# A Mamba-2 stage turned round: values as weights, and an order of four engines by hand

## The chip, the cores and the metric

The kernel runs on one core of one Trainium2 chip. The metric is the device time of one execution in microseconds (us), taken as the median of several runs. The profile comes from one execution that a hardware profiler recorded; its engines are PE (matrix products), PEld (loading of weights into PE), DVE, ACT and POOL (elementwise work) and SP (which issues most transfers).

## The reference

One layer of a bidirectional encoder of 1024 positions and 1024 channels. One projection makes the inputs of three branches (Mamba-2, RWKV-7 and HGRN2), which are merged by gates and followed by a feed-forward block. The change is in the Mamba-2 branch alone. All is float32.

```python
def ssd_chunked(x, dt, a, bm, cm):
    ...
    a_cum = jnp.cumsum(dt * a.reshape(G, hg), axis=2)
    xdt = x * dt[..., None]
    seg = a_cum[:, :, :, None] - a_cum[:, :, None]
    ...
    lmat = jnp.exp(jnp.where(mask, seg, -jnp.inf))
    cb = jnp.einsum('bcqgn,bcsgn->bcqsg', cm, bm)
    y_diag = jnp.einsum('bcqsgh,bcsghp->bcqghp', cb[..., None] * lmat, xdt)
    decay_to_end = jnp.exp(a_cum[:, :, -1:] - a_cum)
    chunk_states = jnp.einsum('bcsgn,bcsghp->bcghpn', bm, xdt * decay_to_end[..., None])
    ...
    y_off = jnp.einsum('bcqgn,bcghpn->bcqghp', cm, prev) * jnp.exp(a_cum)[..., None]
    return (y_diag + y_off).reshape(b, L, H, P)

def ssd_branch(z, xbc, dt_raw, conv_w, conv_b, dt_bias, a_log, d_skip, norm_w):
    ...
    y_f = ssd_chunked(xs, dt[:, :, 0], a[0], bm, cm)
    y_b = flip_t(ssd_chunked(flip_t(xs), flip_t(dt[:, :, 1]), a[1], flip_t(bm), flip_t(cm)))
    y = y_f + y_b + xs * d_skip[:, None]
    y = y.reshape(b, L, SSM_INNER) * jax.nn.silu(z)
    return rmsnorm(y, norm_w)
```

There are 16 heads of 64 values in two groups of 8 heads, a state of 128, and 8 chunks of 128 positions.

## The kernel before

The stages run in the order RWKV (`rwkv`), HGRN (`hgrn`), Mamba-2 (`ssd`), merge, feed-forward. The input projection has 79 column tiles. Each is a job (class `Jobs`) of 16 steps, and a step is three matmuls of 128x512 (L330 to L332: high part of the weights by high and low part of x, then low part of the weights by the high part of x). The first two jobs run at the start. The other 77, 3696 matmuls, are dealt out among the stages: `J.fill(n)` puts n steps at that place of the program, `J.share(w)` puts there the share w of what is left, out of `J.weight`, and `J.get` first completes the job whose result it reads. The weights of the stage stand in `FILL["ss"]`. A job also costs ACT a cast (L221) and copies of the result (L272), and DVE or POOL the low part of the weights (`wl`, L223).

A scheduler then makes one row of instructions for each engine. It may bring an instruction ahead of others where its inputs and buffers are there. Inside `tc.manual_schedule(engines=...)` the named engines keep the order of the program instead. Before the change that holds for POOL alone, and only in the chunk loop.

The stage (`ssd`, L1202 to L1438) begins with the step sizes `dt`, their cumulative sums (`cums`, and `cumd` in DRAM, one row for each head and direction) and decays to the chunk's end (`wst`, `dec`). Then, for each of two groups: six convolutions (`conv`: a load, an ACT operation, four DVE operations at L1298, a SiLU), of B, C and four tiles of values; scores `CB` = C·B for each chunk; and transposes (`xps`, L1345) of the values to position-major tiles `xt`.

The chunk loop of a group runs 8 times, with the forward direction at chunk i and the backward one at chunk 7 − i. `pairs` (two steps ahead) loads two exponent tiles of 8x128 per partition (`E<-cumd`), subtracts on POOL (L1368), picks one of the two by the triangle on DVE (L1371), takes exp on ACT and multiplies by `CB` (L1373). Then, for each direction, `yo` (L1389) multiplies C by the state, DVE scales it (`yt`, L1391), POOL adds it to `Y` (L1392); DVE makes weighted values `xw` (L1395), `st` (L1397) multiplies them by B, and POOL (L1401) and DVE (L1402) renew the state. `yd` (L1408) has each head's 128x128 exponent tile as weights and its 64 values as moving data, and L1410 adds it to `Y`, which is position-major. After the loop z is loaded, `Y` is transposed (`ytps`, L1428), gated by SiLU(z), stored in `ysc`, and its squares are summed in `ss`.

The E tiles, the convolutions' tiles and z's share five buffers (`EB`), and the loads of all of them stand in the queue of SP.

Of the kernel before, what the change touches and what calls it, by code (L numbers as in the profile page):

```python
# [9 lines left out]
F32 = mybir.dt.float32  # L10
# [8 lines left out]
P = 128  # L19
# [13 lines left out]
POOL = mybir.EngineType.Pool  # L33

# [5 lines left out]
    "ss": (4, 36, 12, 18, 6, 3, 8, 5, 22, 13, 8),  # L40
# [1161 lines left out]
def ssd(g, xr):  # L1202
# [3 lines left out]
    ysc = g.dram.tile([8, P, L], F32, tag="ysc", name="ysc")  # L1206
    cumd = g.dram.tile([32, L], F32, tag="cumd", name="cumd")
    ss = g.sspool.tile([P, L], F32, tag="ss", name="ss")

    J.weight = F[8] + 2 * F[0] + F[9] + F[10] + 2 * (F[1] + 4 * F[2] + F[3] + 16 * F[4] + 8 * F[5] + F[6] + 4 * F[7])  # L1210
    with ExitStack() as es:
# [12 lines left out]
        ecum = kp.tile([P, NT, 32], F32, tag="ecum", name="ecum")  # L1224
        wst = kp.tile([P, NT, 32], F32, tag="wst", name="wst")
        dec = kp.tile([P, NT, 32], F32, tag="dec", name="dec")
        with tc.tile_pool(name="s0t", bufs=1) as tp:
# [12 lines left out]
            J.share(F[8])  # L1240
# [29 lines left out]
            nc.scalar.activation(ecum, cums, AF.Exp)  # L1270
# [6 lines left out]
            nc.vector.tensor_sub(cums, cums, ld)  # L1277
# [7 lines left out]
        m8 = kp.tile([P, P], U8, tag="m8", name="m8")  # L1285
        nc.vector.tensor_copy(m8, mlt)

# [18 lines left out]
        for grp in range(2):  # L1306
            with ExitStack() as es2:
# [7 lines left out]
                J.share(F[1] + F[9] * grp)  # L1315

                cbd = yp.tile([P, NT], F32, tag="cbd", name="cbd")
                for h in range(2):
                    ps = pp.tile([P, 4, P], F32, tag="a", name="cbps", bufs=3)
                    ps2 = pp.tile([P, 4, P], F32, tag="a", name="btps", bufs=3)  # L1320
                    for j in range(4):
# [4 lines left out]
                    dg = yp.tile([P, 4, P], F32, tag="yt", name="dg", bufs=2)  # L1326
# [5 lines left out]
                nc.vector.tensor_tensor(gd, dtT[:, :, 16 + grp * 8:24 + grp * 8],  # L1332
                                        cbd.unsqueeze(2).broadcast_to([P, NT, 8]), MUL)
# [14 lines left out]
                Y = yp.tile([P, NT, 512], F32, tag="Y", name="Y")  # L1348
# [4 lines left out]
                def h3(t):  # L1353
                    return t.rearrange("p (h v) -> p h v", v=64)

                S = [yp.tile([P, 512], F32, tag=f"S{d}", name=f"S{d}") for d in range(2)]
                J.share(F[3])

                def pairs(c):

                    Es = []
                    for d in range(2):
                        e = sp.tile([P, L + 4], F32, tag="E", name="E", bufs=EB)
                        e = e[:, :L].rearrange("p (h t) -> p h t", t=P)
                        nc.sync.dma_start(e, cumd[d * 16 + grp * 8:d * 16 + grp * 8 + 8, c * P:(c + 1) * P]
                                          .unsqueeze(0).broadcast_to([P, 8, P]))
                        cs = cums[:, c, d * 16 + grp * 8:d * 16 + grp * 8 + 8]
                        nc.gpsimd.tensor_tensor(e, e, cs.unsqueeze(2).broadcast_to([P, 8, P]), SUB)  # L1368
                        Es.append(e)
                    e = Es[0]  # L1370
                    nc.vector.copy_predicated(e, m8.unsqueeze(1).broadcast_to([P, 8, P]), Es[1])  # L1371
                    nc.scalar.activation(e, e, AF.Exp)
                    nc.vector.tensor_mul(e, e, CB[:, c:c + 1, :].broadcast_to([P, 8, P]))  # L1373
                    return e

                order = ExitStack()
                order.enter_context(tc.manual_schedule(engines={POOL}))
                nxt = [pairs(0), pairs(1)]
                for i in range(NT):
                    if i < NT // 2:  # L1380
                        for c in (i, NT - 1 - i):
                            nc.gpsimd.tensor_tensor(h3(Y[:, c]), h3(xt[:, c]),
                                                    gd[:, c].unsqueeze(2).broadcast_to([P, 8, 64]), MUL)
                    e = nxt.pop(0)
                    for d in range(2):
                        c = i if d == 0 else NT - 1 - i
                        if i > 0:
                            ps = pp.tile([P, 512], F32, tag="b", name="yo", bufs=2)
                            nc.tensor.matmul(ps, CT[:, c * P:(c + 1) * P], S[d], start=True, stop=True)  # L1389
                            yt = yp.tile([P, 512], F32, tag="yt", name="yt", bufs=2)  # L1390
                            nc.vector.tensor_tensor(h3(yt), h3(ps), per_head(ecum, c, d), MUL)  # L1391
                            nc.gpsimd.tensor_add(Y[:, c], Y[:, c], yt)  # L1392
                        if i < NT - 1:
                            xw = yp.tile([P, 512], F32, tag="xw", name="xw", bufs=2)
                            nc.vector.tensor_tensor(h3(xw), h3(xt[:, c]), per_head(wst, c, d), MUL)  # L1395
                            ps = pp.tile([P, 512], F32, tag="b", name="st", bufs=2)
                            nc.tensor.matmul(ps, Bt[:, c], xw, start=True, stop=True)  # L1397
                            if i == 0:
                                nc.vector.tensor_copy(S[d], ps)
                            else:  # L1400
                                nc.gpsimd.tensor_tensor(h3(S[d]), h3(S[d]), per_head(dec, c, d), MUL)  # L1401
                                nc.vector.tensor_add(S[d], S[d], ps)  # L1402
                        if d == 0 and i + 2 < NT:
                            nxt.append(pairs(i + 2))
                        J.share(F[4])
# [729 lines left out]
```

## Time and profile before

| what | us |
|---|---|
| median of three runs | 2452.01 (2451.94 to 2453.88) |
| the profiled execution | 2453.83 |
| its span | 2452.1 |
| DVE busy in the span | 1611.1 |
| POOL busy in the span | 1078.3 |
| ACT busy in the span | 981.5 |

The span is the stretch from the first to the last instruction. A line of the profile gives the source line, the engine, the operation with the tile written and the tiles read, the count after an x, busy microseconds and mean nanoseconds, then the idle time of the engine before them and what ended it. In a timeline a row begins with start and length in us, and the brackets give the idle time before it and its releaser. A matmul in plain float32 leaves two records, one of the projection leaves one.

### The profile page before, as it was taken

How to read it: one execution, taken by the hardware profiler on the slowest of the kernel's cores; microseconds unless marked ns; L12 is line 12 of the kernel's file. 1: busy time of each engine (PE TensorE's matmuls, PEld its weight loads, DVE VectorE, ACT ScalarE, POOL GpSimd, SP SyncE). 2: the span in 40 equal slices, each digit the busy share in tenths (PEclk: the TensorE clock that was granted, in tenths of full speed). 3: DMA queues.
4: the chain of work that ended last, by engine and by line, in shares of the span. 5: the costliest groups of instructions: out<-in, count | busy, mean ns of one | idle time of the engine just before them, and what ended most of it. 6: DMA issues, size and time to landing. Idle time of an engine off the chain costs nothing.

```text
span 2452.1 us, 37480 instructions
## 1 busy us (share of the span) xinstructions
PE 2288.4 (93%) x14785; PEld 1847.8 (75%) x14785; DVE 1611.1 (66%) x2069; ACT 981.5 (40%) x1428; POOL 1078.3 (44%) x845
## 2 busy tenths in 40 slices
PE   8998999999988998999899889999899999999895
PEld 6776778788767877878668657788688888877674
DVE  5688763455569578546666776652774454479999
ACT  6554532222454655426224245332433333344333
POOL 4433422443136345310751771421464444447985
PEclk9999999999989999999899989999999999999998
DMA  5455685763442232225645646532232222253311
GB/s 150 122 144 133 165 214 123 223 193 109 148 144 87 87 117 74 80 83 173 148 119 169 146 149 212 191 114 76 61 103 87 78 86 86 79 179 116 100 60 69
DMA packets 381212, 306.23 MB, mean 125 GB/s; under 512 B 111273, under 2 KB 323149, under 8 KB 381037
## 3 DMA queue, kind: packets, MB, share of 16 engines
q1 hardware_dynamic: 260909, 225.71, 31.2%
q10 hardware_dynamic: 119936, 77.61, 10.8%
q8 instruction: 116, 1.90, 0.3%
q0 software_dynamic: 192, 0.52, 0.1%
q14 instruction: 59, 0.48, 0.1%
HBM read 209.68 MB, written 94.11 MB: 124 GB/s over the span
## 4 chain that ended last, share of the span: by engine, by line
PE 61%; DVE 23%; POOL 5%; issue 4%; DMA 3%; ACT 3%; SPq 0%; ACTq 0%; DVEq 0%; POOLq 0%
PE mm L330 7%; PE mm L331 7%; PE mm L332 7%; PE ps L1587 6%; PE ps L1589 6%; PE ps L1588 6%; DVE acc L1926 3%; DVE ab L1804 3%; PE mm L232 2%; PE mm L231 2%; PE mm L233 2%; DVE rb L1804 2%; POOL E L1368 2%; PE Gps L807 1%; DMA E<-cumd 1%
## 5 line engine op out<-in xcount | busy, mean ns | idle before, releaser
L330 PE MATMUL mm<-x,wh 128*128 128x512 f32 (+1 forms) x1232 | 500.1, 406 | 0.6 <-ACT wh L221 0.5
L331 PE MATMUL mm<-x,wh 128*128 128x512 f32 (+1 forms) x1232 | 494.4, 401 | 0.0
L332 PE MATMUL mm<-x,wl 128*128 128x512 f32 (+1 forms) x1232 | 492.3, 400 | 0.0
L330 PEld LDWEIGHTS mm<-x,wh 128*128 128x128 f32 (+1 forms) x1232 | 233.8, 190 | 61.9 <-issue 9.7
L332 PEld LDWEIGHTS mm<-x,wl 128*128 128x128 f32 (+1 forms) x1232 | 233.9, 190 | 55.1 <-issue 4.9
L331 PEld LDWEIGHTS mm<-x,wh 128*128 128x128 f32 (+1 forms) x1232 | 234.1, 190 | 53.7 <-issue 6.2
L1587 PE MATMUL ps<-xb,rb 128*128 128x512 f32 x432 | 168.0, 389 | 0.0
L1588 PE MATMUL ps<-xb,rb 128*128 128x512 f32 x432 | 168.0, 389 | 0.0
L1589 PE MATMUL ps<-xb,rb 128*128 128x512 f32 x432 | 167.9, 389 | 0.0
L1587 PE MATMUL ps<-rb,ab 128*128 128x512 f32 x308 | 125.5, 407 | 20.5 <-DVE acc L1926 19.5
L221 ACT CAST wh<-wr 128x1024 fp32r<-128x1024 f32 (+2 forms) x103 | 100.2, 972 | 101.9 <-PE mm L331 86.2
L223 POOL TENSOR_TENSOR wl<-wr,wh 128x1024 fp32r<-128x1024 f32 x30 | 78.9, 2630 | 133.6 <-ACT wh L221 123.1
L223 DVE TENSOR_TENSOR wl<-wr,wh 128x1024 fp32r<-128x1024 f32 (+2 forms) x73 | 98.5, 1349 | 49.6 <-ACT wh L221 49.4
L1588 PE MATMUL ps<-rb,ab 128*128 128x512 f32 x308 | 122.7, 398 | 2.3 <-POOL rb L1804 2.3
L1589 PE MATMUL ps<-rb,ab 128*128 128x512 f32 x308 | 121.5, 397 | 1.5 <-DVE ab L1804 1.5
L1751 ACT CAST rb<-fs 128x512 fp32r<-128x512 f32 x85 | 52.8, 622 | 166.1 <-PE ps L1589 117.8
L272 ACT COPY st<-mm 128x512 f32<-128x512 f32 x130 | 75.5, 582 | 93.2 <-PE mm L332 81.7
L810 DVE TENSOR_TENSOR Gc<-Gps,mk 128x256 f32<-128x256 f32 x64 | 27.2, 424 | 108.2 <-PE Gps L807 62.1
L231 PE MATMUL mm<-oh,wh 128*128 128x512 f32 x224 | 88.5, 397 | 6.1 <-DVE gt L1491 4.2
L1926 DVE TENSOR_TENSOR acc<-acc,ps 128x512 f32<-128x512 f32 x148 | 94.1, 674 | 0.0
L1588 PEld LDWEIGHTS ps<-xb,rb 128*128 128x128 f32 x432 | 81.1, 188 | 16.9
L1589 PEld LDWEIGHTS ps<-xb,rb 128*128 128x128 f32 x432 | 81.1, 188 | 16.8
(503 smaller groups left out, 5472.0 us busy)
## 6 DMA issues: line engine op xcount, KB each, us to landing
wr<-in_w_in_dram ACTq DMA_DIRECT2D x74, 512.0 KB
fr<-in_ffn_w_in_dram SPq DMA_DIRECT2D x44, 512.0 KB
E<-cumd SPq DMA_DIRECT2D x32, 512.0 KB
pg<-st ACTq DMA_DIRECT2D x48, 256.0 KB
gt<-pg SPq DMA_DIRECT2D x24, 512.0 KB
ad<-a SPq DMA_DIRECT2D x22, 512.0 KB
dr<-in_ffn_w_down_dram SPq DMA_DIRECT2D x22, 512.0 KB
ar<-ad SPq DMA_DIRECT2D x22, 512.0 KB
```

What stands on the lines that cost most here:

```text
L221: nc.scalar.copy(hi[:, :kt, :n], raw[:, :kt, :n])
L223: g.lo_eng.tensor_sub(lo[:, :kt, :n], raw[:, :kt, :n], f32(hi[:, :kt, :n]))
L231: nc.tensor.matmul(ps, whi[:, k, :n], xh, start=(k == 0), stop=False)
L272: g.nc.scalar.copy(st[:n], ps)
L330: g.nc.tensor.matmul(ps[:n], w[0][:, k, :n], xh, start=(k == 0), stop=False)
L331: g.nc.tensor.matmul(ps[:n], w[0][:, k, :n], xl, start=False, stop=False)
L332: g.nc.tensor.matmul(ps[:n], w[1][:, k, :n], xh, start=False, stop=(k == KT - 1))
L1587: nc.tensor.matmul(ps, ah, bh, start=(i == 0), stop=False)
L1588: nc.tensor.matmul(ps, ah, bl, start=False, stop=False)
L1589: nc.tensor.matmul(ps, al, bh, start=False, stop=(i == n - 1))
L1804: eng.tensor_sub(blk[:, 1], s, f32(blk[:, 0]))
L1926: nc.vector.tensor_add(m[j], m[j], ps)
```

## The change

Inside the stage, for each group:

- `yd` has the values as weights (128x64) and the exponent tile of the head as moving data (128 columns). Even heads write to the lower half of the partitions, odd heads to the upper. The result is feature-major: 128 partitions hold two heads' values, and the free axis has 4 pairs of heads by 128 positions. `yo` has quarters of the state as weights and C as moving data, so it has the same shape.
- So `Y`, the position-major scaling by `ecum` and the transposes at the end are gone. The feature-major scaling is `X`, the exp of half of the loaded rows (ACT), by which DVE multiplies `yo`. The D skip goes into the diagonal of the exponent tile, which a second copy_predicated (`id8`, `gd`) sets.
- z is loaded and SiLU'd ahead of the loop, stored in `zd`, and read back chunk by chunk (`gate`); `ysc` is stored chunk by chunk.
- The subtraction of `cums` from the two exponent tiles on POOL becomes eight ACT operations with a bias for the forward one, and stays on POOL for the backward one. The product of the state and `dec` moves from POOL to DVE.
- All seven backward states (`Sb`) are made first; then one loop over the chunks does both directions.
- From the first exponents to the loop's end, PE, ACT, DVE and POOL all keep the order of the program. The weights in `FILL["ss"]` are new.

```diff
-    "ss": (4, 36, 12, 18, 6, 3, 8, 5, 22, 13, 8),
+    "ss": (4, 30, 12, 5, 5, 14, 22, 8, 5),
...
-    J.weight = F[8] + 2 * F[0] + F[9] + F[10] + 2 * (F[1] + 4 * F[2] + F[3] + 16 * F[4] + 8 * F[5] + F[6] + 4 * F[7])
+    J.weight = F[6] + 2 * F[0] + F[7] + F[8] + 2 * (F[1] + 4 * F[2] + 7 * F[3] + 8 * F[4] + 8 * F[5])
...
-            nc.vector.tensor_sub(cums, cums, ld)
+            nc.vector.tensor_sub(cums, ld, cums)
...
+        m8, id8 = (kp.tile([P, P], U8, tag=n, name=n) for n in ("m8", "id8"))
         nc.vector.tensor_copy(m8, mlt)
+        nc.vector.tensor_copy(id8, g.ident)
...
+                nc.vector.tensor_add(gd, dtT[:, :, grp * 8:grp * 8 + 8], dtT[:, :, 16 + grp * 8:24 + grp * 8])
+                nc.vector.tensor_tensor(gd, gd, cbd.unsqueeze(2).broadcast_to([P, NT, 8]), MUL)
...
-                Y = yp.tile([P, NT, 512], F32, tag="Y", name="Y")
+                for q in range(grp * 4, grp * 4 + 4):
+                    zs = sp.tile([P, L + 4], F32, tag="E", name="zs", bufs=EB)[:, :L]
+                    nc.sync.dma_start(zs, J.get(g.pz, q))
+                    nc.scalar.activation(zs, zs, AF.Silu)
+                    nc.sync.dma_start(zd[q], zs)
...
-                def pairs(c):
...
+                        h0 = d * 16 + grp * 8
+                        nc.sync.dma_start(e, cumd[h0:h0 + 8, c * P:(c + 1) * P].unsqueeze(0).broadcast_to([P, 8, P]))
                         Es.append(e)
+                    return Es
+                def exponents(c, Es):
+                    Xs = []
+                    for d in (1, 0):
+                        e, h0 = Es[d], d * 16 + grp * 8
+                        X = yp.tile([P, 4, P], F32, tag=f"X{d}", name="X", bufs=2)
+                        if c != (0, NT - 1)[d]:
+                            for b in range(2):
+                                hr = slice(b * 64, b * 64 + 64)
+                                nc.scalar.activation(X[hr], e[hr, b::2], AF.Exp)
+                        cs = cums[:, c, h0:h0 + 8]
+                        if d == 0:
+                            for h in range(8):
+                                nc.scalar.activation(e[:, h], e[:, h], AF.Identity, bias=cs[:, h:h + 1])
+                        else:
+                            nc.gpsimd.tensor_tensor(e, e, cs.unsqueeze(2).broadcast_to([P, 8, P]), ADD)
+                        Xs.insert(0, X)
+                    return Xs
+                def pick(Es):
+                    nc.vector.copy_predicated(Es[0], m8.unsqueeze(1).broadcast_to([P, 8, P]), Es[1])
+                def decays(c, e):
+                    nc.scalar.activation(e, e, AF.Exp)
+                    yield
+                    nc.vector.tensor_mul(e, e, CB[:, c:c + 1, :].broadcast_to([P, 8, P]))
+                    nc.vector.copy_predicated(e, id8.unsqueeze(1).broadcast_to([P, 8, P]),
+                                              gd[:, c].unsqueeze(2).broadcast_to([P, 8, P]))
+                    yield
+                def gate(c):
+                    z = yp.tile([P, 4, P], F32, tag="z", name="z", bufs=2)
+                    nc.sync.dma_start(z, zd[grp * 4:grp * 4 + 4, :, c * P:(c + 1) * P].rearrange("q p t -> p q t"))
+                    return z
...
+                Sb = yp.tile([P, NT - 1, 512], F32, tag="Sb", name="Sb")
+                Sa = yp.tile([P, 512], F32, tag="Sa", name="Sa")
+                def weighted(d, c):
+                    xw = yp.tile([P, 512], F32, tag="xw", name="xw", bufs=2)
+                    nc.vector.tensor_tensor(h3(xw), h3(xt[:, c]), per_head(wst, c, d), MUL)
+                    return xw
+                def update(d, c, xw, old, new):
+                    ps = pp.tile([P, 512], F32, tag="b", name="st", bufs=2)
+                    nc.tensor.matmul(ps, Bt[:, c], xw, start=True, stop=True)
+                    if old is None:
+                        nc.vector.tensor_copy(new, ps)
+                    else:
+                        nc.vector.tensor_tensor(h3(new), h3(old), per_head(dec, c, d), MUL)
+                        nc.vector.tensor_add(new, new, ps)
+                order = ExitStack()
+                order.enter_context(tc.manual_schedule(engines={PE, ACT, DVE, POOL}))
+                Es = rows(0)
+                X, z = exponents(0, Es), gate(0)
+                ahead = rows(1)
+                xw = weighted(1, NT - 1)
+                pick(Es)
+                for _ in decays(0, Es[0]):
+                    pass
+                for c in range(NT - 1, 0, -1):
+                    xn = weighted(1, c - 1) if c > 1 else weighted(0, 0)
+                    update(1, c, xw, Sb[:, c] if c < NT - 1 else None, Sb[:, c - 1])
+                    xw = xn
+                    J.share(F[3])
+                for i in range(NT):
+                    ts = slice(i * P, (i + 1) * P)
+                    nEs = ahead
+                    if i + 2 < NT:
+                        ahead = rows(i + 2)
+                    if i + 1 < NT:
+                        nX, nz = exponents(i + 1, nEs), gate(i + 1)
+                    part = []
+                    for d, S in ((1, Sb[:, i] if i < NT - 1 else None), (0, Sa if i else None)):
+                        if S is None:
+                            continue
+                        ps = pp.tile([P, 4, P], F32, tag="b", name="yo", bufs=2)
+                        for q in range(4):
+                            nc.tensor.matmul(ps[:, q], S[:, q * P:(q + 1) * P], CT[:, ts], start=True, stop=True)
+                        nc.vector.tensor_mul(X[d], X[d], ps)
+                        part.append(X[d])
+                    if i < NT - 1:
+                        update(0, i, xw, Sa if i else None, Sa)
+                    J.share(F[4])
...
+                    ps = pp.tile([P, 4, P], F32, tag="a", name="yd", bufs=3)
                     for h in range(8):
-                        nc.tensor.matmul(ps[:, h], e[:, h], xt[:, i, h * 64:h * 64 + 64],
+                        nc.tensor.matmul(ps[h % 2 * 64:h % 2 * 64 + 64, h // 2], xt[:, i, h * 64:h * 64 + 64], e[:, h],
                                          start=True, stop=True)
-                    nc.vector.tensor_add(Y[:, i], Y[:, i], ps.rearrange("p h v -> p (h v)"))
+                    y = part[0]
+                    if len(part) > 1:
+                        nc.vector.tensor_add(y, y, part[1])
+                    nc.vector.tensor_add(y, y, ps)
+                    nc.vector.tensor_mul(z, z, y)
+                    nc.sync.dma_start(ysc[grp * 4:grp * 4 + 4, :, ts].rearrange("q p t -> p q t"), z)
...
+                    nc.scalar.activation(y, z, AF.Square)
+                    nxt = iter(())
+                    if i + 1 < NT:
+                        pick(nEs)
+                        nxt = decays(i + 1, nEs[0])
+                        next(nxt)
+                    if i + 2 < NT:
+                        xw = weighted(0, i + 1)
+                    eng = nc.vector if grp and i == NT - 1 else nc.gpsimd
+                    eng.tensor_add(y[:, 0:2], y[:, 0:2], y[:, 2:4])
+                    if grp == 0:
+                        eng.tensor_add(ss[:, ts], y[:, 0], y[:, 1])
+                    else:
+                        eng.tensor_add(y[:, 0], y[:, 0], y[:, 1])
+                        eng.tensor_add(ss[:, ts], ss[:, ts], y[:, 0])
+                    next(nxt, None)
                     J.share(F[5])
+                    if i + 1 < NT:
+                        Es, X, z = nEs, nX, nz
```

The rows of PE, up to the last product of HGRN's states (`sps`), are the same before and after. The next place is in the setup of group 0, where the step sizes are transposed (`dtps`; `mm` is a matmul of the projection). Before, on PE:

```order
L330 MATMUL mm<-x_373,wh 128x512
L1246 MATMUL dtps<-ident,dt 128x32 x8
L331 MATMUL mm<-x_374,wh 128x512
L332 MATMUL mm<-x_373,wl 128x512
L330 MATMUL mm<-x_382,wh 128x512
L331 MATMUL mm<-x_383,wh 128x512
L332 MATMUL mm<-x_382,wl 128x512
L330 MATMUL mm<-x_391,wh 128x512
L1246 MATMUL dtps<-ident,dA 128x32 x8
```

The same place after, on PE, with the norm of HGRN's last head (`nps`) ahead of it:

```order
L179 MATMUL nps<-t,ones 128x512
L180 MATMUL nps<-t,ones 128x512
L1247 MATMUL dtps<-ident,dt 128x32 x8
L1247 MATMUL dtps<-ident,dA 128x32 x8
L1258 MATMUL rps<-tri_le,dAT 32x128 x4
L1258 MATMUL rps<-tri_ge,dAT 32x128 x4
```

No matmul of the projection stands there any more. The end of that setup, on PE, after: the last scores and transposes, the first product of a backward state (`st`), and behind it the first projection matmuls since HGRN's `sps`:

```order
L1324 MATMUL cbps<-CT,BT 128x128 x4
L1325 MATMUL btps<-ident,BT 128x128 x4
L1346 MATMUL xps<-ident,xq 128x128 x32
L1420 MATMUL st<-xw,Bt 128x512
L331 MATMUL mm<-x_217,wh 128x512
L332 MATMUL mm<-x_218,wh 128x512
L333 MATMUL mm<-x_217,wl 128x512
```

Counted over PE's rows, 2562 projection matmuls stood ahead of that `sps` before and 2553 after. Ahead of the first `st` stood 3055 before, and 2553 after; the others moved behind it.

The last place is the start of the chunk loop of group 0, on DVE. Before:

```order
L1395 TENSOR_TENSOR xw<-xt,wst 128x512
L1371 COPY_PREDICATED E<-m_10226,E 128x1024
L1395 TENSOR_TENSOR xw<-xt,wst 128x512
L1373 TENSOR_TENSOR E<-E,CB 128x1024
L1371 COPY_PREDICATED E<-m_10226,E 128x1024
L1399 COPY S_10668<-st 128x512
```

After, with `id` the mask of the diagonal and `Sb` the backward states:

```order
L1415 TENSOR_TENSOR xw<-xt,wst 128x512
L1393 COPY_PREDICATED E<-m_10222,E 128x1024
L1399 TENSOR_TENSOR E<-E,CB 128x1024
L1400 COPY_PREDICATED E<-id_10223,gd 128x1024
L1415 TENSOR_TENSOR xw<-xt,wst 128x512
L1422 COPY Sb<-st 128x512
```

The second weighted values, which the second `st` needs, stand behind the whole exponent tile of chunk 0 now, with the new operation on the diagonal among it; before, only the pick stood between them.

77 lines of the change are left out of this document (6 added, 71 removed).

## The prediction

> **What bounds the kernel now.** I read the page first: its share of busy time and the chain that ended last.
>
> ```profile
> span 2452.1 us, 37480 instructions
> ...
> PE 61%; DVE 23%; POOL 5%; issue 4%; DMA 3%; ACT 3%; SPq 0%; ACTq 0%; DVEq 0%; POOLq 0%
> ```
>
> PE ends the chain for 61% of the span, so the Mamba-2 stage must be judged by what PE loses in it. I cut the stage into stretches: from the last HGRN state matmuls at 1022 us to the first use of the exponents (1173.3), the chunk loop of group 0, the setup of group 1, its loop, and the start of the merge. The columns are the engines' busy time (and instructions), the granted TensorE clock, the DMA share and GB/s.
>
> ```profile
> core 0: us, PE busy (x) PEld busy (x) DVE busy (x) ACT busy (x) POOL busy (x), PEclk, DMA share, GB/s
> 1022.00:1173.30 151.30, 146.12 (x918) 122.34 (x917) 82.58 (x95) 66.53 (x87) 26.41 (x30) 0.98 0.39 118
> 1173.30:1285.00 111.70, 99.43 (x410) 71.30 (x409) 77.26 (x70) 26.49 (x30) 79.84 (x48) 0.91 0.55 131
> 1285.00:1366.00 81.00, 81.00 (x403) 68.22 (x402) 52.75 (x48) 39.36 (x49) 13.89 (x18) 1.00 0.54 167
> 1366.00:1461.90 95.90, 75.66 (x289) 49.90 (x287) 72.25 (x67) 27.95 (x30) 78.00 (x47) 0.84 0.54 139
> 1461.90:1500.00 38.10, 38.09 (x177) 31.95 (x178) 28.37 (x34) 20.05 (x23) 5.04 (x3) 0.96 0.78 268
> sum 478.00, PE 440.30 PEld 343.72 DVE 313.21 ACT 180.38 POOL 203.19; mean PE 88.06 PEld 68.74 DVE 62.64 ACT 36.08 POOL 40.64
> ```
>
> In both setups PE is full although almost nothing of the stage itself runs on it: 146 of 151 us and 81 of 81. What fills it are the projection jobs. In the two loops PE waits and its clock falls, while POOL is busy 80 of 112 us and 78 of 96. The work by line, same 478 us, and the true step of a matmul:
>
> ```profile
> L331 PE MATMUL mm<-x,wh 128*128 128x512 f32 x381 | 156.5, 411 | 0.0
> L330 PE MATMUL mm<-x,wh 128*128 128x512 f32 x381 | 156.3, 410 | 0.0
> L332 PE MATMUL mm<-x,wl 128*128 128x512 f32 x382 | 154.9, 406 | 0.0
> L1389 PE MATMUL yo<-S,CT 128*128 128x512 f32 x56 | 37.0, 752 | 20.0 <-DVE S L1399 12.3 <-DVE yt L1391 5.5 <-DVE S L1402 2.1
> L1408 PE MATMUL yd<-xt,E 128*128 128x64 f32 x256 | 36.2, 295 | 0.0
> L1397 PE MATMUL st<-xw,Bt 128*128 128x512 f32 x56 | 33.5, 682 | 10.7 <-DVE yt L1391 5.3 <-DVE S L1402 3.0 <-DVE S L1399 2.2
> L231 PE MATMUL mm<-oh,wh 128*128 128x512 f32 x49 | 19.3, 401 | 1.9 <-ACT oh L1466 1.9
> L1428 PE MATMUL ytps<-ident,Y 128*128 128x128 f32 x64 | 9.1, 295 | 0.0
> ...
> 1165.15 0.39 PE L332 MATMUL mm<-x,wl 128*128 128x512 f32 x1
> 1165.37 0.39 PE L330 MATMUL mm<-x,wh 128*128 128x512 f32 x1
> ...
> 1277.33 1.02 PE L1389 MATMUL yo<-S,CT 128*128 128x512 f32 x2
> 1177.80 1.89 PE L1408 MATMUL yd<-xt,E 128*128 128x64 f32 x16
> 1024.00 3.29 PE L1145 MATMUL sps<-Vt,t 128*128 128x128 f32 x28
> ```
>
> Records overlap: a projection matmul lasts 0.39 us but the next one starts 0.23 later (0.2275 over long runs), so 0.16 of every length is overlap. A yo or st (two records each) then takes 0.86, a yd (two records) 0.23, a 128x128 record 0.11. Work at full clock: 1144 projection records and 145 of the merge (three lines, 49 the first) by 0.2275 = 293 us; yo and st 112 by 0.43 = 48; yd 256 by 0.116 = 30; ytps 64 by 0.11 = 7; the rest of the 2197 records, scores, transposes and HGRN's last products, about 36. Sum 414. The stretch lasts 478, so **PE loses 64 us now**: 38 idle by the sum row, the rest at a low clock.
>
> **The change, part by part.** It removes PE work and POOL work, and it moves projection work. Less PE work first. The 64 ytps records go: −7 us. Then yd gets weights of 64 columns (the values) in place of 128, in alternate halves of the array, with 128 moving columns in place of 64. The nearest row has such halves:
>
> ```profile
> 1055.01 1.15 PE L1108 MATMUL vps<-lv 128*64 128x64 f32 x32
> 1056.09 0.50 PE L332 MATMUL mm<-x,wl 128*128 128x512 f32 x1
> ```
>
> These are 16 matmuls of 64 moving columns (two records each), and the next matmul starts 1.08 us after them, so each takes 0.0675; 128 moving columns double that to 0.135, my value. The lower bound is 0.107, the upper 0.22, as for a 128x128 matmul (two records by 0.11) with no overlap of halves. 128 matmuls by 0.23 − 0.135 is −12 us, with −16 and −1 as the ends. By the Trainium skill, "TensorEngine Tiling (Array Packing)", section Performance Considerations, a weight of at most 64 columns allows up to twice the rate; the vps row agrees, and by that rule the term would be 0.107 and −15, three us from mine. y_off by quarters of S moves as many columns as before: ±0. New PE sum: 414 − 19 = **395**.
>
> Now the move. Until HGRN's last sps the rows of PE are the same, and 2553 projection matmuls of 3696 have been issued there (2562 before). Before, the scheduler then put 293 more ahead of the first dtps and 493 ahead of the first st (3055). With the change that number is 0: PE is one of the ordered engines now, later jobs belong behind the loop's first st, and nothing may cross it. So PE has only the stage's own chain from 1022 until the backward pass gets going, and 114 us of projection (about 500 by 0.2275) that ran there must run later. How long is that starved chain? Rows of the present setup, with what they waited for in brackets:
>
> ```profile
> 1066.12 0.74 DVE L1162 COPY_PREDICATED scd<-msk,vps 128x512 f32<-128x512 uint8 x1 [5.35 <-PE vps L1108]
> 1078.09 0.75 DVE L1184 SCALAR_TENSOR_TENSOR t<-ops,vcolsv,gg 128x512 f32<-128x512 f32 x1 [5.13 <-PE ops L1181]
> 1086.67 0.75 DVE L1184 SCALAR_TENSOR_TENSOR t<-ops,vcolsv,gg 128x512 f32<-128x512 f32 x1 [5.48 <-PE ops L1181]
> 1097.84 0.69 DVE L1196 TENSOR_TENSOR t<-t 128x512 f32<-128x512 f32 x1 [6.25 <-ACT t L1195]
> ...
> 1110.23 1.29 DVE L1298 SCALAR_TENSOR_TENSOR acc<-pt,vcolsv,acc 128x1024 f32<-128x1024 f32 x1 [3.09 <-ACT acc L1296]
> 1155.82 5.32 DVE L1298 SCALAR_TENSOR_TENSOR acc<-pt,vcolsv,acc 128x1024 f32<-128x1024 f32 x4 [0.89 <-ACT acc L1296]
> 1161.17 1.06 ACT L1300 ACTIVATE xq<-acc 128x1024 f32<-128x1024 f32 x1 [0.46 <-DVE acc L1298]
> 1166.43 1.23 DVE L223 TENSOR_TENSOR wl<-wr,wh 128x1024 fp32r<-128x1024 f32 x1 [5.30 <-ACT wh L221]
> 1164.57 1.90 POOL L1368 TENSOR_TENSOR E<-E,cums 128x1024 f32<-128x1024 f32 x1 [15.23 <-DMA E<-cumd]
> 1171.37 1.90 POOL L1368 TENSOR_TENSOR E<-E,cums 128x1024 f32<-128x1024 f32 x1 [4.90 <-DMA E<-cumd]
> 1173.30 1.32 DVE L1371 COPY_PREDICATED E<-m,E 128x1024 f32<-128x1024 uint8 x1 [4.38 <-POOL E L1368]
> ...
> 1162.26 18.70 DMA E<-cumd
> ```
>
> HGRN's tail runs from 1024.0 to 1098.5, 74.5 us. The first three rows wait 16 us for PE, whose own matmuls there last 1 to 3 us and sit between projection matmuls; with the smaller waits I take off 24, so 50. From there to the first conv operation it takes 11.7 us for loads, unchanged. The convs run from 1110.2 to 1161.1, 50.9 us; five wl splits of 1.23 leave DVE and some waits behind projection go, so 43. From the last conv to the first st (now 12) transposes no longer queue behind projection: 7. First st at 1024 + 112 = about 1136. There PE would be free, but DVE's rows now stand as follows: first weighted values, then pick, the product with CB and the diagonal of chunk 0, and only then the values of the second st. Those need both exponent tiles. Their loads now stand on SP behind four z loads, and the second behind a z store that frees its buffer; the load in the last row took 18.7 us. I put the end of the second load at 1145 (an estimate: loads land 6.8 us apart in the two L1368 rows, and a z store goes ahead of this one). Then come half the tile's exp twice, 1.2, the biases, 1.9 (POOL's L1368 row for the same sum), pick, 1.3 (the COPY_PREDICATED row), exp, 1.1 (ACT's row of 128x1024), the product and the diagonal, 1.2 and 1.3 (DVE's rows of 128x1024), and the values, 0.7: **second st at about 1155**. PE work in these 133 us is about 32 (30 of the rest, the first st, little of projection): **101 us lost**. Bounds: 1137 with the loads in time, or 1167 as slow as now.
>
> The clock falls in such stretches: the rows of the loops have 0.91 and 0.84 with gaps of a few us. The Trainium skill, "TensorE: Matmul & The Clock Gate", Part 1, has the clock halved after an idle window of about 3.4 us; the rows agree. By it, the 32 us of PE work in the starved stretch would cost up to twice, at worst +12 if the chain waits for all of it.
>
> Afterwards there is more projection than before: 471, 201 and 471 matmuls in group 0's loop, group 1's setup and its loop. A chunk has 46 of them (10.5), st 0.86, yo 1.7, yd 1.1: 14.2 us of PE. DVE has two or three products with yo and sums, gating, pick, exponents, and wl:
>
> ```profile
> L1395 DVE TENSOR_TENSOR xw<-xt,wst 128x512 f32<-128x512 f32 x13 | 19.8, 1524 | 0.0
> L1371 DVE COPY_PREDICATED E<-m,E 128x1024 f32<-128x1024 uint8 x8 | 17.5, 2186 | 18.0 <-POOL E L1368 18.0
> ...
> L1368 POOL TENSOR_TENSOR E<-E,cums 128x1024 f32<-128x1024 f32 x14 | 30.5, 2196 | 7.9 <-DMA E<-cumd 7.9
> L1392 POOL TENSOR_TENSOR Y<-Y,yt 128x512 f32<-128x512 f32 x14 | 19.7, 1410 | 19.5 <-DVE yt L1391 19.5
> ```
>
> Beside a busy POOL, xw takes 1.52 and pick 2.19; alone, 0.68 and 1.32 (1173.30). POOL loses the S and Y operations and one of two exponents: 3.5 us of a chunk are left, so most of DVE runs at the short length: seven of 0.69, one 0.7, 1.3, 1.2, 1.3 and 1.2 for wl, 10.5 to 12. That, ACT's eight small biases and two half exponents (8 of 14), and z and ysc by DMA (512 KB a chunk more; the last window carried 268 GB/s) lie beside PE; if PE's cover went, the excess over 14.2 would show. I add 6 for waits at the loops' ends, 2 for the clock after the starved stretch, 2 at the merge: 10.
>
> **Sum.** 395 + 101 + 10 = 506 against 478: +28. The profiled execution lasted 2453.83 (span 2452.1), and the median of the three runs is 1.8 lower, 2452.01. I put +28 on the median: **2480 us**. Own range: 2452 (loads in time, loops without loss, yd at 0.107) to 2515 (yd at 0.22, +11; starved stretch +12; POOL contention on DVE half the time, +12).
>
> **Rivals.** First, **DVE binds the loops**: every operation at its length beside POOL makes 18 us of a chunk against 14.2, 16 chunks by 3.7 = +59: 2539. For it speaks that the pick row had POOL beside it; against it that POOL loses two thirds of its time.
>
> Second, **faster**, the other side: the starved stretch is mostly PE's own queue delay. If tail and convs shorten further and the exponents are ready, the second st comes by 1125: 395 + 71 + 4 = 470, −8: 2444. The loops' old loss of 64 us really goes, so this decides as soon as the second st is before about 1130. Against it speaks DVE: its 82.6 busy us in the first stretch are nearly all chain, and the loads come on top.
>
> Third, **no change**: a second st between 1130 and 1137 with small losses, 2452; PE has merely lost elsewhere what it lost in the loops.
>
> **How the numbers follow.** Forecast 0.60, DVE bound 0.10, faster 0.20, no change 0.10. One measurement here tells about 0.2%, 5 us. Faster 0.20, same 0.10, slower 0.70. The range goes from 2440, which takes in the second rival, to 2520; it leaves out the first.
>
> **What would show it.** The PE row of the starved stretch: some 30 us busy in 130, clock well under 1, and no projection lines between sps and st. The second st near 1155, its idle ended by DVE's xw; behind it pick ended by a load. In the loops PE above 95%, xw at 0.7, 14 us a chunk, yd's eight matmuls in 1.1. It is wrong if the second st starts before 1137, if loop chunks take 18 us with PE waiting for DVE, or if yd still takes 1.9.

## The result, and the profile after

The changed kernel takes 2593.8 us (median of 4 runs, 2589.61 to 2596.09), the kernel before 2452.41: ratio 1.0574, 95% interval 1.0555 to 1.0592, or +141 us where +28 was forecast. The sign was right, the size was not, and the time lies outside the range.

The page's span and the chain that ended last, by engine:

```profile
span 2594.0 us, 37935 instructions
...
PE 54%; DVE 25%; DMA 8%; ACT 5%; issue 5%; POOL 2%; SPq 1%; ACTq 0%; DVEq 0%; POOLq 0%
```

PE's share of the chain fell from 61 to 54%, and transfers rose from 3 to 8. The windows of the changed kernel are cut at its own events: second st (1172.3), first yd (1202.9), last yd of group 0 (1338.4), second st of group 1 (1422.1), first and last yd of group 1. Columns as in the prediction.

```profile
core 0: us, PE busy (x) PEld busy (x) DVE busy (x) ACT busy (x) POOL busy (x), PEclk, DMA share, GB/s
1022.00:1172.30 150.30, 53.32 (x443) 44.94 (x441) 77.55 (x92) 53.57 (x73) 26.70 (x29) 0.62 0.33 87
1172.30:1202.90 30.60, 28.19 (x108) 20.02 (x108) 14.50 (x22) 8.37 (x17) 2.04 (x1) 0.95 0.36 89
1202.90:1338.40 135.50, 113.03 (x573) 88.64 (x572) 83.34 (x87) 60.61 (x110) 27.44 (x26) 0.90 0.52 129
1338.40:1422.10 83.70, 69.11 (x319) 56.86 (x320) 38.67 (x39) 36.75 (x53) 4.29 (x9) 0.90 0.62 174
1422.10:1451.60 29.50, 26.66 (x109) 19.12 (x107) 13.94 (x21) 8.37 (x17) 2.04 (x1) 1.00 0.35 92
1451.60:1588.60 137.00, 110.18 (x573) 86.44 (x572) 77.39 (x80) 55.37 (x106) 34.19 (x27) 0.91 0.45 122
```

The setup of group 0 is starved as forecast: PE busy for 53 of 150 us, at a clock of 0.62, where it was 146 of 151. What was not forecast are the two loops: 136 and 137 us, PE idle for 22 and 27 of them and at 0.90 and 0.91 of its clock on average, and no other engine near full.

For all kernels of this study I made one count: the records of PE in a stage times the unit prices of the prediction (0.2275 a projection matmul, 0.43 for 512 columns of a two-record product, 0.116 and 0.0675 a yd record before and after). A stage's length less that work is what PE **lost** there. A setup ends at the second st (or, before the change, at the second st of the loop), and the backward pass is counted with it.

| us lost by PE | setup 0 and backward pass | loop 0 | setup 1 and backward pass | loop 1 | sum |
|---|---|---|---|---|---|
| before | 8 | 21 | 0 | 29 | 58 |
| changed kernel | 120 | 36 | 20 | 37 | 213 |

The kernel before runs one more st and four yo behind its last yd of group 1 and loses 5 more there, so its stage loses 63 in all (the 64 of the prediction). That makes 150 more lost in the stage. The first 49 us of the merge lose 8 more than before (10 against 2), and PE has 17 us less work by the same count. 150 + 8 − 17 = 141, as measured. A stage's length is its work and its loss by definition, so this sum shows no cause; it says where the time went.

Against the kernel before, 112 came in setup 0, 20 in setup 1 and 18 in the loops. Against the forecast the loops stand out. Of the 113 us by which it was short, about 19 lie in setup 0 (120 against 101), 20 in setup 1 (none forecast) and 73 in the loops and the merge's start (83 against the 10 forecast for both).

### The profile page after: what moved, and what is told of

Read it like the earlier page. It is cut to its first block, busy times and chain, and to the rows that moved or that the text cites. A ratio compares the mean times of both kernels' runs of the same rounds, so it can differ in the third digit from the quotient of the medians.

```text
span 2594.0 us, 37935 instructions
## 1 busy us (share of the span) xinstructions
PE 2292.0 (88%) x14889; PEld 1856.7 (72%) x14889; DVE 1626.0 (63%) x2125; ACT 1045.4 (40%) x1610; POOL 970.4 (37%) x793
## 4 chain that ended last, share of the span: by engine, by line
PE 54%; DVE 25%; DMA 8%; ACT 5%; issue 5%; POOL 2%; SPq 1%; ACTq 0%; DVEq 0%; POOLq 0%
PE ps L1643 6%; PE ps L1645 6%; PE ps L1644 6%; PE mm L331 6%; PE mm L332 5%; PE mm L333 5%; DMA wr<-in_w_in_dram 3%; DVE ab L1860 2%; DVE acc L1982 2%; PE mm L232 2%; PE mm L233 2%; PE mm L234 2%; DVE wl L224 1%; DVE lv L1045 1%; DVE rb L1860 1%
## 5 line engine op out<-in xcount | busy, mean ns | idle before, releaser
L331 PE MATMUL mm<-x,wh 128*128 128x512 f32 (+1 forms) x1232 | 516.9, 420 | 0.6 <-ACT wh L222 0.5
L332 PE MATMUL mm<-x,wh 128*128 128x512 f32 (+1 forms) x1232 | 492.8, 400 | 0.0
L331 PEld LDWEIGHTS mm<-x,wh 128*128 128x128 f32 (+1 forms) x1232 | 237.3, 193 | 68.9 <-issue 16.6
L332 PEld LDWEIGHTS mm<-x,wh 128*128 128x128 f32 (+1 forms) x1232 | 237.0, 192 | 57.4 <-issue 9.9
L224 DVE TENSOR_TENSOR wl<-wr,wh 128x1024 fp32r<-128x1024 f32 (+2 forms) x73 | 91.7, 1257 | 163.0 <-ACT wh L222 152.8
L1420 PE MATMUL st<-xw,Bt 128*128 128x512 f32 x56 | 40.0, 804 | 92.5 <-DVE X L1455 47.6
L1387 POOL TENSOR_TENSOR E<-E,cums 128x1024 f32<-128x1024 f32 x16 | 34.1, 2129 | 160.6 <-ACT X L1381 160.6
```

Of the source, the lines that this page charges most:

```text
L224: g.lo_eng.tensor_sub(lo[:, :kt, :n], raw[:, :kt, :n], f32(hi[:, :kt, :n]))
L331: g.nc.tensor.matmul(ps[:n], w[0][:, k, :n], xh, start=(k == 0), stop=False)
L332: g.nc.tensor.matmul(ps[:n], w[0][:, k, :n], xl, start=False, stop=False)
```

## Experiments

Each kernel ran once beside a run of the kernel before on the same chip, unless an interval is given. The kernel before took 2448.5 to 2458.0 us in these runs, so a few us between two single runs say nothing.

### Whose order it is

**e1**: the changed kernel, POOL alone held to the program's order.

```diff
-                order.enter_context(tc.manual_schedule(engines={PE, ACT, DVE, POOL}))
+                order.enter_context(tc.manual_schedule(engines={POOL}))
```

> The changed kernel with POOL alone in the order of the program, as before the change; PE, ACT and DVE are left to the scheduler. It has 503 projection matmuls between HGRN's last sps and the first st, where the changed kernel has none. Theory A, the order costs it (no projection in the setups, and in the loops the cast and the split of the weights stuck behind their load): nearly all of the 141 us comes back, 2430 to 2470 us. Theory B, the turned-round computation costs it (yo and st share two PSUM buffers, the exponent tile stands ahead of the second st): only the starved setup of 116 us is filled, the loops go on losing 70 us, 2500 to 2530 us.

Measured: 2483.2 us, before 2458.0. 111 of the 141 us come back, not all. Lost: 19 in setup 0, 21 in loop 0, 6 in setup 1, 64 in loop 1. The setups are full of projection again, and the last loop has hardly any left: 24 of its matmuls stand there. The time lies between the two theories, nearer to A, and it shows a third thing: freed, the turned-round kernel is still 25 us slower than the one before.

**e2**: the kernel before, held to the program's order on four engines.

```diff
-                order.enter_context(tc.manual_schedule(engines={POOL}))
+                order.enter_context(tc.manual_schedule(engines={PE, ACT, DVE, POOL}))
```

> The kernel before with PE, ACT, DVE and POOL in the order of the program in its chunk loops, nothing else. 57 projection matmuls are left between HGRN's last sps and the first st, and before there were 493. Theory A: slower than before by about 100 (setup) plus 40 or more (pinned casts in the loops), 2560 to 2620 us. Theory B: the loops of before lose no more than now, and only the setup is starved, at most 2550 us.

Measured: 2659.3 us, before 2458.0: +201, more than either theory gave. Lost: 102, 77, 12, 68. The order alone, without any of the new computation, costs more than the whole change. The waits of all engines in its first loop (engine and line, what it waited for, us in total, times, longest):

```profile
POOL Y L1393 <- DVE yt L1392: 127.0, 14, 17.3
PEld st L1398 <- DVE xw L1396: 71.5, 12, 18.0
PE st L1398 <- DVE xw L1396: 61.5, 12, 17.2
...
DVE wl L224 <- ACT wh L222: 47.0, 6, 10.7
ACT wh L222 <- DMA wr<-in_w_in_dram: 40.3, 6, 10.4
```

PE waits 61 us for DVE, DVE 47 us for the cast of the projection's weights, and the cast 40 us for their load. Of these the last is the start of a chain that the kernel before, left to the scheduler, doesn't have: in its first loop the wl of DVE wait 1.3 us for casts, and the casts for no load.

### What the loops wait for

The changed kernel shows the same chain in its first loop. First the waits, then one chunk in time (start, length, operation; "..." marks lines left out, of the projection and of other engines).

```profile
DVE wl L224 <- ACT wh L222: 40.1, 5, 8.9
ACT wh L222 <- DMA wr<-in_w_in_dram: 31.2, 6, 7.1
...
PE st L1420 <- DVE X L1455: 22.5, 6, 5.9
```

```profile
1219.83 0.33 ACTq L274 DMA_DIRECT2D pg<-st  x1
1220.19 0.45 ACTq L220 DMA_DIRECT2D wr<-in_w_in_dram  x1
...
1224.55 1.05 ACT L222 CAST wh<-wr 128x1024 fp32r<-128x1024 f32 x1 [4.75 <-DMA wr<-in_w_in_dram]
1225.63 1.23 DVE L224 TENSOR_TENSOR wl<-wr,wh 128x1024 fp32r<-128x1024 f32 x1 [7.80 <-ACT wh L222]
1226.78 0.68 DVE L1467 TENSOR_TENSOR X<-X 128x512 f32<-128x512 f32 x1
1227.57 0.69 DVE L1468 TENSOR_TENSOR X<-X,yd 128x512 f32<-128x512 f32 x1
1228.29 0.69 DVE L1469 TENSOR_TENSOR z<-z,X 128x512 f32<-128x512 f32 x1
1228.90 1.33 DVE L1393 COPY_PREDICATED E<-m,E 128x1024 f32<-128x1024 uint8 x1
...
1231.35 1.37 DVE L1399 TENSOR_TENSOR E<-E,CB 128x1024 f32<-128x1024 f32 x1
...
1232.76 1.30 DVE L1400 COPY_PREDICATED E<-id,gd 128x1024 f32<-128x1024 uint8 x1
...
1233.94 1.27 DVE L1455 TENSOR_TENSOR X<-X,yo 128x512 f32<-128x512 f32 x2
1234.68 1.12 PE L1420 MATMUL st<-xw,Bt 128*128 128x512 f32 x2 [2.59 <-DVE X L1455]
```

ACT issues the load of a job's weights and, as the program has it, casts them next; the bytes take 4.4 us, and ACT stands still. The low part on DVE stands next in DVE's row and waits too, 7.8 us here, although X and z behind it have nothing to do with the projection. From the cast on, DVE works without a gap for nine microseconds, and only at the end comes the product with yo, whose buffer in PSUM (the memory into which PE writes) the next st needs. PE, with 45 to 48 projection matmuls a chunk, runs out before that.

**e4**: in this stage the load is issued one job earlier, nothing else.

```diff
...
-        return load_w(g, g.A["w_in"][0][:, job.c0:job.c0 + job.n], KT, job.n)
+        w = load_w(g, self.src(i), KT, job.n, raw=self.raws.pop(i, None))
+        if self.early and i + 1 < len(self.jobs):
+            self.raws[i + 1] = load_raw(g, self.src(i + 1), KT, self.jobs[i + 1].n)
+        return w
...
+    J.early = True
```

> The changed kernel, but in the Mamba-2 stage the load of a job's weights is issued one job earlier (behind the cast of the job before), so that the cast pinned behind it finds its data there. Same order of everything else. Theory A, the cast waits for its load and holds up DVE and then PE: the 31 us that ACT waits for weights in the loop of group 0 go, and the loss of both loops falls from 73 to about 35: about 2555 us. Theory B, the shared PSUM buffers alone: no change, 2585 to 2600 us.

Measured: 2519.3 us, before 2458.0: 74 us less than the changed kernel, more than theory A gave. Windows of its two loops:

```profile
1198.60:1303.50 104.90, 102.18 (x573) 82.11 (x572) 80.87 (x85) 61.23 (x112) 26.62 (x26) 1.00 0.63 167
...
1412.70:1514.70 102.00, 102.00 (x573) 82.13 (x573) 74.32 (x80) 54.74 (x106) 34.42 (x27) 1.00 0.64 156
```

Same 573 records of PE, 105 and 102 us in place of 136 and 137, PE busy for 102 us of each at full clock. In the first loop the cast's wait for its load is gone from the view of waits, and wl waits for casts that stand behind other work, at most 3.4 us at a time:

```profile
DVE wl L229 <- ACT wh L227: 15.7, 6, 3.4
```

The loops lose 5 and 2 us: **nearly all that they lost came from one load issued too late in two rows that may not move.**

**e3**: ACT and DVE left to the scheduler, PE and POOL held; and **e12**: DVE alone left to it.

```diff
-                order.enter_context(tc.manual_schedule(engines={PE, ACT, DVE, POOL}))
+                order.enter_context(tc.manual_schedule(engines={PE, POOL}))
```

> The changed kernel with PE and POOL in the order of the program and ACT and DVE left to the scheduler. PE's row in group 0 is the same as in the changed kernel. Theory A: the starved setup stays (116 us lost), but the casts and splits no longer stand in the way in the loops, whose loss falls from 73 to below 35: 2545 to 2560 us. Theory B: the loops lose as much as now, 2585 to 2600 us.

Measured: 2528.2 us, before 2458.0. The loops lose 17 and 3; setup 0 with its backward pass 109 (the exponent tile no longer stands ahead of the second st). PE's row from the first st to the end of loop 0 is the same; what changed is who stands behind the cast. Better than theory A gave.

> The changed kernel with PE, ACT and POOL in the order of the program and DVE left to the scheduler; weights loaded late, as in the changed kernel. The cast on ACT still stands right behind its load, but the split on DVE may stand behind other work. If it is DVE's row that hands the wait on to PE: the loops lose below 25 of their 73 us, and the second st comes at about 1147, together 2520 to 2540 us. If ACT's row alone is enough (exponents, copies and the square behind the cast): the loops still lose 50 or more, 2560 to 2580 us.

Measured: 2534.5 us, before 2455.3. The time and the second st, at 1144.3, are as expected if DVE's row hands the wait on. But the loops lose 20 and 22, together 42, which lies between the two expectations; ACT still waits 28 us for weights in the first of them. So by these two runs freeing DVE's row takes 31 of the 73 us away, and freeing ACT's as well another 22 (42 to 20 in e3).

**e5**: the rival, that st waits for one of the two PSUM buffers that it shares with yo: it takes one of yd's three instead.

```diff
-                    ps = pp.tile([P, 512], F32, tag="b", name="st", bufs=2)
+                    ps = pp.tile([P, 512], F32, tag="a", name="st", bufs=3)
```

> The changed kernel, but st takes its PSUM buffers from the three of yd's, so that it no longer waits until DVE has read a yo out of the shared two. Theory A, the casts pinned behind their load hold up DVE: the wait moves to the next matmul that DVE feeds, no gain, 2580 to 2600 us. Theory B, the shared buffers: the 47.6 us that PE waits ahead of st for the product with yo go, about 2550 us.

Measured: 2616.4 us, before 2455.6: 22 slower than the changed kernel, where B gave some 40 less and A no gain, 2580 to 2600. The releaser in the profile changes its name only; of PE's waits in the first loop, nearly all are:

```profile
PE st L1420 <- DVE xw L1415: 36.0, 5, 9.3
```

st now waits for its weighted values, which stand behind the same split in DVE's row. Why it waits longer there was not tried, and st with buffers that it shares with nobody was not tried either. But the kernel with early loads keeps the two shared buffers, and its loops lose 5 and 2: that "PE st" waited for "DVE X" named the last of a chain, not its cause.

### What the setup waits for

The longest wait of PE in the starved setup, and the chain that ended there, in the changed kernel:

```profile
PE st L1420 <- DVE xw L1415: 25.1, 2, 23.1
PE xps L1346 <- ACT xq L1301: 19.9, 3, 7.5
PE vps L1109 <- DVE lv L1047: 19.7, 4, 11.1
```

```profile
1140.58 1.07 ACT zs L1352
1141.66 9.82 DMA zd<-zs
1151.55 11.31 DMA E<-cumd
1162.88 0.63 ACT X L1381
1163.52 0.63 ACT X L1381
1164.17 2.45 ACT E L1385 x8
1166.70 1.30 DVE E L1393
1168.03 1.06 ACT E L1397
1169.12 1.24 DVE E L1399
1170.38 1.30 DVE E L1400
1171.67 0.58 DVE xw L1415
1172.30 2.08 PE st L1420 x2
```

The second exponent tile takes over the buffer of a z tile, so z's store (9.8 us) and the load (11.3) follow each other, and then come the small operations, 9.4 us (10 forecast), but 17 us later than forecast.

**e6**: e4, and the exponent tile of chunk 0 behind the backward pass.

```diff
-                pick(Es)
-                for _ in decays(0, Es[0]):
-                    pass
                 for c in range(NT - 1, 0, -1):
...
                     J.share(F[3])
+                pick(Es)
+                for _ in decays(0, Es[0]):
+                    pass
```

> The kernel with the early weight loads (2519 us), and the exponent tile of chunk 0 (pick, exp, product, diagonal) moved behind the backward pass on DVE and ACT. If the exponent tile was what the second st waited for: second st at about 1145 in place of 1169, some 25 us in group 0 and 8 in group 1, 2486 us. Rival: the wait only moves to the first yd behind the backward pass, and the time stays at 2510 to 2520 us.

Measured: 2506.7 us, before 2455.6. The second st comes at 1148.7 (1169.5 in e4), but only 13 us stay: the first yd comes 13.4 us earlier (1185.2 in place of 1198.6), since the exponent tile is late for it too: pick starts at 1178.3 there and the diagonal ends at 1185. Between the two expectations.

**e7** and **e8**: other shares of the projection, 321 matmuls ahead of the first st; e7 on e4, e8 on e6.

```diff
-    "ss": (4, 30, 12, 5, 5, 14, 22, 8, 5),
+    "ss": (4, 90, 20, 4, 2, 6, 22, -83, 5),
```

> The kernel with the early weight loads (2519 us), and other shares of the projection: 321 of its matmuls between HGRN's last sps and the first st (none now), 24 in a chunk in place of 45. If the starved setup is the rest of the loss: PE's 114 us lost there fall to about 45, the loops lose some 25 us each since DVE binds them at 11 us a chunk, about 2490 us. Rival: the projection in the setup delays the chain as it did before, and what is won there is lost again: 2515 us or more.

> Both together: early weight loads, exponent tile of chunk 0 behind the backward pass, and the new shares. If the gains add up, 2465 us; if the exponent tile is late anyway, as in the run with the shares alone.

Measured: 2502.4 and 2490.5 us, before 2455.6. e7 lies between its expectations: setup 0 with the backward pass loses 70 (117 in e4), the loops 29 and 16. The gains measured one by one add up: 13 for e6 and 17 for e7 against e4, 29 for both together in e8; the 2465 of the expectation took both gains for larger. In e8 setup 0 with the backward pass loses 57 (103 in e6), and the loops 30 and 16 (5 and 2). The setup took 75 us of projection (330 by 0.2275) and grew by 27, from 126.7 to 153.8 us, since the scheduler put all of it ahead of the first scores (cbps), in the way of HGRN's last products: the last of HGRN's norms (nps) starts at 1097.9 (1074.8 in e6). That is the other face of the starved setup: without projection the chain itself runs faster.

**e9**: fewer in the setup, 30 in a chunk (on e8). **e10**: e9, with the exponent rows ahead of z.

```diff
-    "ss": (4, 90, 20, 4, 2, 6, 22, -83, 5),
+    "ss": (4, 65, 20, 4, 3, 7, 22, -70, 5),
```

```diff
+                Es = rows(0)
                 for q in range(grp * 4, grp * 4 + 4):
                     zs = sp.tile([P, L + 4], F32, tag="E", name="zs", bufs=EB)[:, :L]
...
-                Es = rows(0)
```

> The kernel of the last run (early weight loads, exponent tile behind the backward pass, projection in the setup; 2490.5 us), with 24 projection matmuls of each setup and some 40 of each loop dealt the other way: 249 between HGRN's last sps and the first st, 30 in a chunk. The loops lost 30 and 16 us there because DVE's chain of 10 to 12 us a chunk is longer than PE's 8.5; with 30 PE has 10.5. Expected: loops lose 20 less, the setup 10 more, 2480 us. If it stays at 2490, the stage's own chain (setup, backward pass, eight chunks) is the bound, however the projection is dealt.

> As the balanced kernel, with the exponent rows of chunk 0 loaded ahead of the four z tiles instead of behind them. If their load is what the first yd behind the backward pass waits for: 14 us less in group 0, about 2466 us. Rival: the buffers, shared with the z tiles, only make z late: no change against the balanced kernel.

Measured: e9 2509.9 us, ratio to before 1.0234 (1.0215 to 1.0253); e10 2491.6 us, ratio 1.0164 (1.0149 to 1.0179). e9 missed: the loops lost 27 and 16, nearly as in e8 (30 and 16), and setup 0 with the backward pass 75 (57 in e8, 67 expected); why it lost so much more was not found. e10 gives 18 less than e9, more than expected of the step, but the base was off, and it ends where e8 did. Projection dealt out differently moves the loss between stages; none of these kernels comes near the 58 us that the one before loses.

**e11**: early weight loads in the kernel before (the edit of e4).

> The kernel before with the early weight loads. There ACT and DVE are not held to the program's order, so the cast need not stand right behind its load: no change, 2445 to 2460 us. If early loads are worth something on their own, 2440 us or less.

Measured: 2452.7 us, ratio 1.0001 (0.9991 to 1.0012): no change. The rows of ACT in the first loop of the kernel before say why:

```profile
1201.65 1.48 ACTq L219 DMA_DIRECT2D wr<-in_w_in_dram  x1
...
1220.94 1.03 ACT L221 CAST wh<-wr 128x1024 fp32r<-128x1024 f32 x1
```

Left to the scheduler, the cast stands 19 us behind the load, with other work ahead of it, and waits for nothing.

## Why the prediction was wrong

**The account was right on PE's work.** 19 us less were forecast and 17 counted. Nearly all that was missed is PE's loss, so the question is only where the waits were mis-sized.

**The starved setup was right, and too small.** Forecast: 2553 matmuls at sps and none before the first st, 101 us lost, second st at 1155. Measured: 116 lost up to the second st at 1172.3. HGRN's tail came out at 54 us (forecast 50) and the first st at 1142.9 (1136). The term that was mis-sized is the load of the second exponent tile: forecast to end at 1145, it ended at 1163, since the z store ahead of it took 9.8 us and itself 11.3. "As slow as now", 1167, stood in the text as the upper bound, and was passed.

**The failed step is "I add 6 for waits at the loops' ends", with the sentence ahead of it** that wl and the rest "lie beside PE". It costed wl as 1.2 us of DVE's work and never asked what the wl row waits for once DVE and ACT may not pass it. The prediction counted instructions by engine and added durations; it had wl among the operations of a chunk, but what stands ahead of wl is a cast, and ahead of the cast a load, with 4.2 to 6.7 us from its issue to the cast in loop 0. In the loops PE lost 73 us in place of the few forecast, and 66 of them go in e4, with the same operations and only the load issued earlier. Part of the loss is the clock: PE is idle for 22 us in loop 0 and loses 36, and a granted clock of 0.90 over 135.5 us makes the other 14.

**Setup 1 was left out.** Its z store (14.4 us on the chain) and z load (10.0) stand ahead of the exponents as in setup 0: 17 us there and 3 in its backward pass, none forecast.

**The yd term was right.** Eight matmuls with the values as weights, then the next matmul of PE:

```profile
1220.79 1.09 PE L1463 MATMUL yd<-E,xt 128*64 128x128 f32 x16
1221.82 0.50 PE L331 MATMUL mm<-x,wh 128*128 128x512 f32 x1
```

1.03 us for eight is 0.129 each, 0.135 forecast and 0.23 before. The rule of the Trainium skill ("TensorEngine Tiling (Array Packing)", Theoretical Speedup) is up to twice the rate, which the prediction estimated as 0.107. Against the 0.23 before, the 0.129 here is 1.8 times.

**The rivals.** "DVE binds the loops" came nearest in time (2539) and had the place right, DVE's row, but not the mechanism: most of DVE's operations ran at the short lengths (pick 1.31 and the product with yo 0.68 in the mean of loop 0; xw, 1.21, was between), and DVE was busy for 83 of 135 us. It waited. The prediction's own sign of being wrong, chunks of 18 us with PE waiting for DVE, came true: six of the seven distances from one yd to the next in loop 0 are 18 to 23 us. The faster rival's point of decision, a second st before 1130, was never near.

**What stays open.** Why the turned-round stage, freed (e1) or mended (e8, e10), remains 25 to 40 us behind the kernel before was not settled by one experiment. The lengths say this much: backward pass and loop of a group take 104 to 134 us in e1, e8 and e10, against 94 and 88 us for the loop before, also where PE has little to do in them (101 projection matmuls, 23 us, in the 125 us of e1's second group). That points to a longer chain of the stage itself, on which saved PE work buys nothing, but no run measured that chain alone. An order with ACT alone left to the scheduler was not tried. No version beat the kernel before; the best of the turned-round ones was e1 at 2483.2 us, one run.

## What to carry to other kernels

When an engine is put under a fixed order, every instruction of other work that stands in its row becomes a wait for the whole row: read for each of them what it waits for (here a load issued just ahead of it), not how long it runs. Work that a scheduler used as filler in a starved stretch does not follow by itself into a stretch of fixed order; count how much of it stands in each stage before and after. And if the loads are moved ahead of their use by one step, the same fixed order can cost almost nothing in the loop.

## What the runs showed of the hardware

An idle stretch of 2 us can halve PE's clock, and a longer one need not. In the changed kernel, ahead of the st at 1215.39:

```profile
1212.40 1.06 PE L1454 MATMUL yo<-CT,Sa 128*128 128x128 f32 x8
1215.39 1.22 PE L1420 MATMUL st<-xw,Bt 128*128 128x512 f32 x2 [1.94 <-DVE X L1455]
...
1216.84 0.63 PE L332 MATMUL mm<-x,wh 128*128 128x512 f32 x1
1217.26 0.63 PE L333 MATMUL mm<-x,wl 128*128 128x512 f32 x1
```

After 1.94 us of idling the projection matmuls start 0.42 us apart until 1219.4, then 0.23 again. So these 1.9 us of waiting cost some 1.7 more by the clock. The next idle stretch of the same loop, 2.59 us ahead of the st at 1234.68, did not lower it. Windows of both stretches and of what follows each:

```profile
1213.46:1215.39 1.93, 0.00 (x0) 0.00 (x1) 1.92 (x3) 1.87 (x4) 1.10 (x1) 1.00 0.52 72
1216.30:1219.70 3.40, 3.40 (x9) 2.61 (x8) 1.43 (x2) 2.18 (x7) 0.19 (x1) 0.50 0.67 120
1232.09:1234.68 2.59, 0.00 (x1) 0.01 (x1) 2.56 (x4) 2.38 (x4) 1.09 (x1) 1.00 0.33 73
1234.68:1238.10 3.42, 3.42 (x13) 2.51 (x14) 2.33 (x3) 3.11 (x10) 1.09 (x1) 1.00 0.45 96
```

The other four idle stretches of this loop that are longer than 1 us, 2.9 to 5.9 us, all brought half clock. So the idle window that the prediction names for the clock is not a bound below which a wait is free, and its "the rows agree" holds only in part. What decides between 1.9 and 2.6 us was not tried.
